# A two-branch decoder layer on one core: single-transfer attention operands, outputs split where they are made, a state update that adds in PSUM

## The chip, the cores and the metric

One core of a Trainium2 chip runs one program. The metric is device time in microseconds, the median of three runs, lower is better. The engines are TensorE (PE: matmuls, with PEld for its weight loads), VectorE (DVE), ScalarE (ACT), GpSimd (POOL), and SyncE (SP), which here only issues DMAs.

## What is computed

One layer on 2048 tokens of width 1024, in float32. A normalised and modulated input goes through one projection (4232 columns). Half of its heads are a recurrence (RWKV-7), half a causal attention with a forget-gate bias. Both are gated and go through one output projection and a second normalisation.

```python
proj = h @ w_in
rw = rw + (rw_prev - rw) * rwkv_mix            # token mix: with the token before
# recurrence, 8 heads of 64, per token t (S is 64x64 per head)
sa = einsum('bhvk,bhk->bhv', S, kk_t)
S = S * w_t - sa * b_t + v_t * k_t             # outer products
y = einsum('bhvk,bhk->bhv', S, r_t)
# attention, 8 heads of 64
s = einsum('bhqd,bhkd->bhqk', qb, kh) * scale + cb[..., None] - cum[:, :, None, :]
p = softmax(where(causal, s, -inf))
# both, then
y = concatenate([y_a, y_b]) * silu(gate)
out = y @ w_out
return layer_norm(alpha * x + (1 + gate_c) * out, ln_g, ln_b)
```

## The kernel before

**Precision.** The large products are taken on operands split in two parts, a rounded high part and the rest (low), with three matmuls (high x high, high x low, low x high) per product; those operands have the type fp32r. The recurrence runs in full float32, where one matmul in the program is two records in the trace.

**Stages.** The sequence is cut into two halves of 1024 tokens, and these into blocks of 512 (`NB`). `proj_stream` runs the projection for a half, tile by tile of 128 output columns (weights arrive by DMA in `wst`, `weights` splits them into `wsp` with one ACT and one POOL instruction). `proc_stream` runs the recurrence and then the attention of each half, while projection matmuls (`ps<-ht,wsp` in the trace) fill PE beside them. At the end the output projection runs over 16 tiles of 128 tokens (`final_tile`, `final_x`, `final_evac`), with its weights' place, `wsp`, now holding the transposed layer output, read back from DRAM (`yscr`).

**Recurrence.** `rwkv_stream` takes 8 units per half (4 pairs of heads by 2 blocks). A unit's 8 chunks of 64 tokens first need a triangular solve (`rwkv_solve`, small matmuls of 32 rows and columns), then `rwkv_batch` (line 1407) runs for two chunks at a time: four matmuls of 128 rows and 128 columns combine the solved factors (`X`) with the right sides (`Z`); ACT and DVE take the result out of PSUM into `Fh` (one half of it through DVE with an addition, the rest copied by ACT). Then, in strict order, each chunk: `mm` for the next state and `mm` for the output, two of each, one per head, and two DVE instructions that scale the new state by `dl`, the chunk's decay, into the other state buffer. A chunk can begin only when the one before has written its state. In `state` each head's 64 rows lie beside a 64x64 identity in the other 64 rows, so that one matmul over 128 rows adds what the chunk itself brings:

```python
for h in range(2):
    i = 2 * h + ci
    mm(b.ap[hs(h), 0:64], Fh[:, i, 64:128], cur[:, h, :])
```

**Attention.** `ev_fox` splits q and k of a block into high and low parts and stores them in DRAM (`qscr`, `kscr`), `ev_f` stores the cumulative forget gates in three parts (`cscr`). `fox_ops` (line 1640) loads the operands of each head and block back with `conv`: each operand (`q1`, `k1`: 64 rows and 3 rows for the bias; `q2`, `k2`: two times 64 rows) is two DMAs into one tile of `fx_s`. `fox_values` loads and transposes the value blocks (`arena<-vscr`). `fox_s` computes scores, `fox_exp` the exponentials, `fox_pv` the products with the values, `fox_out` (line 1853) normalises, gates, and stores an output block in `yscr`; `rwkv_post` (line 1465) does so for the recurrence.

**What sets the order.** The program is written by concurrent generators, and a model of the chip (class `Driver`: `cost`, `on_pe`, `time`) decides which generator issues next, so the modelled durations set the order of all instructions on each engine. The order is fixed when the program is built. All instructions pass through one helper, so all have line 134 in the trace; they are told apart by tile names.

Of the kernel before, what the change touches and what calls it, by code (L numbers as in the profile page):

```python
# [9 lines left out]
F32 = mybir.dt.float32  # L10
# [3 lines left out]
OP = mybir.AluOpType  # L14
# [3 lines left out]
D = 1024  # L18
# [119 lines left out]
class Driver:  # L138
# [31 lines left out]
    def cost(self, e, op, ops, kw):  # L170
# [3 lines left out]
        if "dma_start" in op:  # L174
            return 450.0 if e.name == "sp" else 1000.0
# [35 lines left out]
    def on_pe(self, t, op, ops):  # L211
# [6 lines left out]
        if nr == nc == 4:  # L218
            d = max(stream + (14 if n >= 256 else 3), load + 2)
        else:  # L220
            d = max(stream + (load if nc < 4 else 6), 25.0)
# [113 lines left out]
def hymba_kernel(ctx: ExitStack, tc, x, c, emb_ln_g, emb_ln_b, w_ada, b_ada, w_in, rwkv_mix, w0,  # L335
# [10 lines left out]
    def dap(t, offset, ap):  # L346
# [36 lines left out]
    yscr = [dram.tile([D, TB], F32, name=f"yscr{i}") for i in range(2)]  # L383
    cscr = [dram.tile([3, 8, TB], F32, name=f"cscr{i}") for i in range(2)]
    fscr = [{k: [dram.tile([2, 128, TB] if k in "qk" else [128, TB], F32, name=f"{k}scr{h}{i}") for i in range(4)]
             for k in "qkvg"} for h in range(2)]
    qscr1 = dram.tile([3, 512], F32, name="qscr1")
# [31 lines left out]
    state = const.tile([128, 2, 4, 2, 64], F32, name="state")  # L419
# [156 lines left out]
    def start_consts():  # L576
# [57 lines left out]
        qr = yield from slots.get()  # L634
# [24 lines left out]
        for b in range(2):  # L659
            for p in range(4):  # L660
                dve.tensor_copy(state[64:128, b, p, 0, :], i64[64:128, :])
                dve.tensor_copy(state[0:64, b, p, 1, :], i64[0:64, :])
            yield
# [200 lines left out]
    def weights():  # L864
# [4 lines left out]
        while True:  # L869
# [7 lines left out]
            if k == "out":  # L877
                hf, t0 = divmod(p * 128, TB)
                sp.dma_start(wst[:, 0], dap(yscr[hf], t0, [[TB, 128], [128 * TB, KT], [1, 128]]))
                drv.spawn(final_x(p), 0)  # L880
            else:
                sp.dma_start(wst[:, 0], dap(w_in, c0, [[4232, 128], [128 * 4232, KT], [1, 128]]))
# [64 lines left out]
    def shift_mix(b, g, o):  # L947
# [5 lines left out]
        dve.scalar_tensor_tensor(o[:, 0:1], car[:, g:g + 1], par("mix", g), o[:, 0:1],  # L953
                                 op0=OP.mult, op1=OP.add)
# [11 lines left out]
    def ev_f(b, half, blk):  # L966
# [47 lines left out]
        for t in (z, e, u):  # L1014
            t.free()

# [20 lines left out]
    def ev_fox(k):  # L1037
        def ev(b, half, p, blk):
# [9 lines left out]
            else:  # L1048
# [5 lines left out]
                i = int(k == "q")  # L1054
                sp.dma_start(to[i, :, cols], s.ap)
                yield
                sp.dma_start(to[1 - i, :, cols], l.ap)
                l.free()
            if k in "vg":
                sp.dma_start(to[:, cols], s.ap)  # L1060
# [346 lines left out]
    def rwkv_batch(p, n, c0, bufs, u, qt, yb, dl, st):  # L1407
# [6 lines left out]
        Xh = xs.ap.rearrange("p (i c) -> p i c", c=128)  # L1414
# [13 lines left out]
        for i in range(4):  # L1428
            o = 2 * (i % 2) + i // 2
            mm(b.ap[:, o * 128:(o + 1) * 128], Xh[:, i, :], Z[:, i, :])  # L1430
        yield
        bf = b.ap.rearrange("p (i c) -> p i c", c=128)
        for h in range(2):
            i = slice(2 * h, 2 * h + 2)
            tt(Fh[hs(h), i, 0:64], bf[hs(h), i, 0:64], kr[hs(h), g, 1], OP.add)
            tt(Fh[hs(h), i, 64:128], bf[hs(h), i, 64:128], i64[hs(h), None, :].to_broadcast([64, 2, 64]), OP.add)
        for h in range(2):
            o = hs(1 - h)
            i = slice(2 * h, 2 * h + 2)
            act.activation(Fh[o, i, :], bf[o, i, :], AF.Copy)  # L1440
# [4 lines left out]
        for ci in range(2):  # L1445
# [4 lines left out]
            for h in range(2):  # L1450
                i = 2 * h + ci
                mm(b.ap[hs(h), 0:64], Fh[:, i, 64:128], cur[:, h, :])
            with drv.side():
                for h in range(2):
                    i = 2 * h + ci
                    mm(yb.ap[hs(h), cc * 64:(cc + 1) * 64], cur[:, h, :], Fh[:, i, 0:64])
            yield
            ts(nxt[0:64, 0, :], b.ap[0:64, 0:64], dl[0:64, cc:cc + 1], None, OP.mult)
            ts(nxt[64:128, 1, :], b.ap[64:128, 0:64], dl[64:128, cc:cc + 1], None, OP.mult)
# [3 lines left out]
        st["next"] = (n, c0 + 2) if c0 + 2 < 8 else (n + 1, 0)  # L1463

    def rwkv_post(half, p, blk, yb, bonus):
# [29 lines left out]
        g.free()  # L1495
        yield
        sp.dma_start(yscr[half][p * 128:(p + 1) * 128, blk * NB:(blk + 1) * NB], Y.ap)
        Y.free()
        yield
# [35 lines left out]
    def rwkv_stream(half):  # L1535
# [20 lines left out]
        def elems():  # L1556
            for n in range(8):
# [8 lines left out]
                u.amuse = 2  # L1566
                u.done = done
# [72 lines left out]
    def fox_ops(half, st):  # L1640


        def conv(key, o, H, name, b4):
            while (b4 // 2, H // 2, name[0] + "f", b4 % 2) not in res:
                yield 0
            src = fscr[b4 // 2][name[0]][H // 2]
            c = (b4 % 2) * NB
            if name[1] == "2":
                for i in range(2):
                    sp.dma_start(o.f[hs(i)], src[i, hs(H % 2), c:c + NB])  # L1650
            else:
                sp.dma_start(o.f[0:64], src[int(name == "q1"), hs(H % 2), c:c + NB])
                sp.dma_start(o.f[64:67], cscr[b4 // 2][:, H, c:c + NB] if name == "k1" else qscr1)
# [12 lines left out]
    def fox_guard(half, st):  # L1666
# [15 lines left out]
        def finish(H, qg, mx, left):  # L1682
# [20 lines left out]
            sp.dma_start(ops[H, "q1", qg].f[64:65].rearrange("o (j x) -> o j x", j=4), mrow[0:4, r].bitcast(F32))  # L1703
# [149 lines left out]
    def fox_out(half, p, h, qi, nk, pv, o, sums):  # L1853
# [43 lines left out]
        g.free()  # L1897
        yield
        sp.dma_start(yscr[half][512 + p * 128:640 + p * 128, qi * NB:(qi + 1) * NB], o.ap)
        o.free()  # L1900
        normed[0] += 1
        yield
# [71 lines left out]
    def final_x(i):  # L1974
# [10 lines left out]
        ts(xt.ap, xt.ap, stats[:, i, 0:1], stats[:, i, 1:2], OP.subtract, OP.mult)  # L1985
        yield
        pool.tensor_tensor(xt.ap, xt.ap, fin["eg"].ap, op=OP.mult)
        yield
        tt(xt.ap, xt.ap, fin["eb"].ap, OP.add)
# [115 lines left out]
```

## Time and profile before

| | |
|---|---|
| median of 3 runs | 1868.69 us (1868.56 to 1870.11) |
| profiled execution | 1866.47 us |
| its span | 1864.7 us |
| PE busy | 1784.5 us (96%), 13609 matmul records |
| DVE busy | 1287.4 us (69%) |
| ACT busy | 804.4 us (43%) |
| POOL busy | 779.3 us (42%) |
| DMA | 181.60 MB, mean 97 GB/s |

The span is the time from the first to the last instruction of one profiled execution. Matmuls on PE overlap, so its busy time counts stretches in which at least one is under way, and from start to start of groups is the safer reading of what a group costs. The granted clock is the share of full speed that TensorE was given in a stretch.

### The profile page before, as it was taken

Reading aid. Unit: us, or ns where it says so; the run is one execution under the profiler, and the core shown is the slowest. Engines: PE = TensorE matmul, PEld = TensorE weight load, DVE = VectorE, ACT = ScalarE, POOL = GpSimd, SP = SyncE. Lnnn points to the kernel's source line nnn. Section 1 sums busy time; section 2 is a strip of 40 time slices with the busy share of each in tenths; the row PEclk is TensorE's granted clock in tenths of the full one; section 3 lists DMA queues with packets and bytes.
Section 4 is the critical chain, followed back from the end, with each engine's and each line's share of the span. In section 5 each row is a group of like instructions: output and inputs, shape, how many; then the busy total and the mean of one; then the engine's idle time right before and its main releaser. Section 6 shows DMA issues by size and latency. Waiting matters only on the chain.

```text
span 1864.7 us, 35565 instructions
## 1 busy us (share of the span) xinstructions
PE 1784.5 (96%) x13609; PEld 1288.3 (69%) x13609; DVE 1287.4 (69%) x3049; ACT 804.4 (43%) x1571; POOL 779.3 (42%) x773
## 2 busy tenths in 40 slices
PE   8999999999999899999999999989899899999995
PEld 6777777767777656677777777767555356666884
DVE  4987685665773768667657675762677584876998
ACT  2454555354444245554554554443244344432000
POOL 1333242422423357743143442424256364566652
PEclk8999999998999999999999999999899899999998
DMA  8252020210122755132021120213422732512433
GB/s 263 72 163 81 30 69 23 80 51 26 53 87 86 226 172 178 58 115 84 19 78 36 41 79 30 75 39 114 131 92 84 244 111 77 191 57 90 153 115 122
DMA packets 172129, 181.60 MB, mean 97 GB/s; under 512 B 12180, under 2 KB 116197, under 8 KB 171960
## 3 DMA queue, kind: packets, MB, share of 16 engines
q1 hardware_dynamic: 171960, 179.33, 30.6%
q8 instruction: 108, 1.77, 0.4%
q14 instruction: 61, 0.50, 0.1%
HBM read 132.10 MB, written 47.13 MB: 96 GB/s over the span
## 4 chain that ended last, share of the span: by engine, by line
PE 55%; DVE 5%; ACT 3%; SPq 3%; DMA 2%; issue 2%; POOL 1%; DVEq 0%; ACTq 0%; POOLq 0%
PE ps L134 55%; SPq L134 3%; ACT rw_s L134 2%; DVE rw_s L134 2%; DMA arena<-vscr 1%; DVE end_s L134 1%; DVE small L134 1%; DVE arena L134 1%; POOL rw_s L134 0%; POOL wsp L134 0%; DMA arena<-in_b_ada_dram 0%; ACT arena L134 0%; DMA yscr<-rw_s 0%; DVE fx_p L134 0%; DMA fx_s<-qscr 0%
## 5 line engine op out<-in xcount | busy, mean ns | idle before, releaser
L134 PE MATMUL ps<-ht,wsp 128*128 128x512 f32 x3840 | 976.4, 400 | 3.4 <-POOL wsp L134 1.3
L134 PEld LDWEIGHTS ps<-ht,wsp 128*128 128x128 f32 x3840 | 701.1, 189 | 163.3 <-issue 15.0
L134 POOL TENSOR_TENSOR wsp<-wst,wsp 128x1024 fp32r<-128x1024 f32 x79 | 192.8, 2440 | 320.2 <-ACT wsp L134 256.2
L134 ACT ACTIVATE rw_s<-ps 64x256 f32<-64x256 f32 (+3 forms) x544 | 215.9, 409 | 200.7 <-PE ps L134 101.0
L134 PE MATMUL ps<-fx_s 67*128 67x512 f32 (+6 forms) x960 | 261.1, 390 | 12.3 <-DMA fx_s<-kscr 4.0
L134 ACT ACTIVATE fx_p<-ps 128x512 f32<-128x512 f32 (+3 forms) x336 | 162.8, 521 | 196.2 <-PE ps L134 175.6
L134 PEld LDWEIGHTS ps<-fx_s 67*128 67x128 f32 (+1 forms) x960 | 165.4, 193 | 118.3 <-issue 47.7
L134 POOL TENSOR_TENSOR fx_p<-fx_p 128x512 f32<-128x512 f32 (+2 forms) x160 | 185.7, 1167 | 140.7 <-PE ps L134 138.3
L134 PE MATMUL ps<-rw_s 32*32 32x32 f32 (+4 forms) x5376 | 227.7, 217 | 17.0 <-DVE rw_s L134 8.0
L134 PEld LDWEIGHTS ps<-rw_s 32*32 32x32 f32 (+3 forms) x5376 | 195.7, 130 | 66.1 <-issue 26.6
L134 DVE TENSOR_TENSOR rw_s<-rw_s 128x24 f32<-128x24 f32 (+11 forms) x544 | 179.8, 336 | 26.0 <-ACT rw_s L134 12.6
L134 DVE TENSOR_REDUCE small<-ps 128x1 f32<-128x512 f32 (+1 forms) x208 | 134.5, 683 | 44.4 <-PE ps L134 43.6
L134 ACT ACTIVATE arena<-ps 128x512 f32<-128x512 f32 (+3 forms) x128 | 74.1, 581 | 191.6 <-PE ps L134 161.7
L134 POOL TENSOR_TENSOR small<-small,nhalf 128x8 f32<-128x8 f32 (+1 forms) x48 | 68.3, 1425 | 211.6 <-DVE small L134 211.5
L134 PE MATMUL ps<-fx_p,fx_v 128*64 128x512 f32 (+3 forms) x640 | 155.9, 556 | 0.0
L134 DVE TENSOR_TENSOR fx_p<-fx_p 128x512 f32<-128x512 f32 (+1 forms) x128 | 111.9, 874 | 51.6 <-POOL fx_p L134 48.9
L134 ACT ACTIVATE wsp<-wst 128x1024 fp32r<-128x1024 f32 x80 | 84.3, 1054 | 134.2 <-PE ps L134 110.1
L134 DVE TENSOR_SCALAR state<-ps,dl 64x64 f32<-64x64 f32 x256 | 72.4, 283 | 64.2 <-PE ps L134 57.2
L134 POOL TENSOR_TENSOR rw_s<-rw_s,arena 128x512 f32<-128x512 f32 x64 | 84.9, 1328 | 69.4 <-ACT arena L134 39.2
L134 DVE TENSOR_TENSOR arena<-ps,arena 128x512 fp32r<-128x512 f32 (+4 forms) x108 | 72.5, 677 | 54.0 <-ACT arena L134 50.3
L134 POOL TENSOR_SCALAR rw_s<-rw_s 64x128 f32<-64x128 f32 x128 | 38.0, 297 | 120.0 <-PE ps L134 109.4
L134 ACT ACTIVATE rw_s<-rw_s 32x256 f32<-32x256 f32 (+2 forms) x112 | 70.0, 653 | 39.4 <-DVE rw_s L134 38.7
(152 smaller groups left out, 1864.9 us busy)
## 6 DMA issues: line engine op xcount, KB each, us to landing
wst<-in_w_in_dram SPq DMA_DIRECT2D x66, 512.0 KB
fx_s<-kscr SPq DMA_DIRECT2D x144, 128.0 KB
fx_s<-qscr SPq DMA_DIRECT2D x96, 128.0 KB
ada_t<-in_w_ada_dram SPq DMA_DIRECT2D x16, 512.0 KB
rw_l<-lowscr SPq DMA_DIRECT2D x32, 256.0 KB
kscr<-arena SPq DMA_DIRECT2D x32, 256.0 KB
qscr<-arena SPq DMA_DIRECT2D x32, 256.0 KB
arena<-in_x_dram SPq DMA_DIRECT2D x16, 512.0 KB
```

Source lines behind the costliest of these rows:

```text
L134: return fn(*args, **kw)
```

## The change

It has six parts.

1. *Recurrence.* The identity rows of `state` go; the tile holds both heads in its 128 rows. What a chunk itself brings to the next state is added in PSUM by two matmuls over 128 rows ahead of the two state matmuls, which now read 64 rows each; the new state is scaled by one DVE instruction for both heads. What the batch's tokens bring to the output is put into the output bank by four matmuls of the batch, to which the chunk's output matmuls add. The batch's four matmuls now make 64 output rows each instead of 128, and two DVE instructions take out what four and two of ACT did.
2. *Attention operands.* The DRAM tiles of q and k hold the bias rows and the parts in the order in which an operand needs them, so that each operand is one DMA (160 in place of 320). For that the high part of q is written twice and the cumulative rows are copied from DRAM to DRAM, and operands wait until that is issued (`res[half, "cum", blk]`).
3. *Outputs.* `store_y` splits each finished output block (32 of them) into high and low, one ACT and one DVE instruction, and stores both; the output weights are then loaded by two DMAs straight into `wsp`, once that buffer is free, with no split by ACT and POOL. `final_x` becomes two DVE instructions in place of two on DVE and one on POOL.
4. *Token mix.* The first column of a block goes from DVE to ACT.
5. *State set-up.* 16 DVE copies into `state` at the start go.
6. *Order model.* SP's modelled cost of a DMA is 600 ns for more than 8 partitions (450 before), and a matmul on a part of the array has another modelled duration. These numbers only move the order.

```diff
-            return 450.0 if e.name == "sp" else 1000.0
+            return (450.0 if list(out.ap)[0][1] <= 8 else 600.0) if e.name == "sp" else 1000.0
...
-            d = max(stream + (load if nc < 4 else 6), 25.0)
+            d = max(stream + 6, load + 5, 52.0)
...
-    yscr = [dram.tile([D, TB], F32, name=f"yscr{i}") for i in range(2)]
+    yscr = [dram.tile([2, D, TB], F32, name=f"yscr{i}") for i in range(2)]
...
-    fscr = [{k: [dram.tile([2, 128, TB] if k in "qk" else [128, TB], F32, name=f"{k}scr{h}{i}") for i in range(4)]
-             for k in "qkvg"} for h in range(2)]
-    qscr1 = dram.tile([3, 512], F32, name="qscr1")
+    rowsof = dict(q=[2, 195, TB], k=[2, 131, TB], v=[128, TB], g=[128, TB])
+    fscr = [{k: [dram.tile(rowsof[k], F32, name=f"{k}scr{h}{i}") for i in range(4)] for k in "qkvg"} for h in range(2)]
+    qscr1 = dram.tile([3, TB], F32, name="qscr1")
...
-    state = const.tile([128, 2, 4, 2, 64], F32, name="state")
+    state = const.tile([128, 2, 4, 64], F32, name="state")
...
-        for b in range(2):
-            for p in range(4):
-                dve.tensor_copy(state[64:128, b, p, 0, :], i64[64:128, :])
-                dve.tensor_copy(state[0:64, b, p, 1, :], i64[0:64, :])
-            yield
...
             if k == "out":
                 hf, t0 = divmod(p * 128, TB)
-                sp.dma_start(wst[:, 0], dap(yscr[hf], t0, [[TB, 128], [128 * TB, KT], [1, 128]]))
+                w = yield from wb.get()
+                for i in range(2):
+                    sp.dma_start(w.ap.bitcast(F32)[:, i], dap(yscr[hf], i * D * TB + t0, [[TB, 128], [128 * TB, KT], [1, 128]]))
                 drv.spawn(final_x(p), 0)
+                yield
+                wready.append((it, w))
+                continue
...
-        dve.scalar_tensor_tensor(o[:, 0:1], car[:, g:g + 1], par("mix", g), o[:, 0:1],
-                                 op0=OP.mult, op1=OP.add)
+        act.activation(o[:, 0:1], car[:, g:g + 1], AF.Identity, scale=par("mix", g), bias=o[:, 0:1])
...
+        for p in range(4):
+            sp.dma_start(dap(fscr[half]["k"][p], blk * NB, [[131 * TB, 2], [TB, 3], [1, NB]]),
+                         dap(cscr[half], 2 * p * TB + blk * NB, [[TB, 2], [8 * TB, 3], [1, NB]]))
+            if blk == 0:
+                sp.dma_start(dap(fscr[half]["q"][p], 0, [[195 * TB, 2], [TB, 3], [1, TB]]),
+                             dap(qscr1, 0, [[0, 2], [TB, 3], [1, TB]]))
+            yield
+        res[half, "cum", blk] = True
...
-                i = int(k == "q")
-                sp.dma_start(to[i, :, cols], s.ap)
+                part = lambda r: dap(to, r * TB + blk * NB, [[rowsof[k][1] * TB, 2], [TB, 64], [1, NB]])
+                sp.dma_start(part(3), s.ap)
                 yield
-                sp.dma_start(to[1 - i, :, cols], l.ap)
+                sp.dma_start(part(67), l.ap)
                 l.free()
+                if k == "q":
+                    sp.dma_start(part(131), s.ap)
...
-        for i in range(4):
-            o = 2 * (i % 2) + i // 2
-            mm(b.ap[:, o * 128:(o + 1) * 128], Xh[:, i, :], Z[:, i, :])
-        yield
-        bf = b.ap.rearrange("p (i c) -> p i c", c=128)
-        for h in range(2):
-            i = slice(2 * h, 2 * h + 2)
-            tt(Fh[hs(h), i, 0:64], bf[hs(h), i, 0:64], kr[hs(h), g, 1], OP.add)
-            tt(Fh[hs(h), i, 64:128], bf[hs(h), i, 64:128], i64[hs(h), None, :].to_broadcast([64, 2, 64]), OP.add)
-        for h in range(2):
-            o = hs(1 - h)
-            i = slice(2 * h, 2 * h + 2)
-            act.activation(Fh[o, i, :], bf[o, i, :], AF.Copy)
+        for ci in range(2):
+            for h in range(2):
+                mm(b.ap[hs(h), ci * 128:ci * 128 + 128], X4[:, ci, 192 * h:192 * h + 64], Z[:, 2 * ci + h, :], start=not ci)
+        for ci in range(2):
+            for h in range(2):
+                xv = X4[:, ci, 64 + 64 * h:128 + 64 * h]
+                mm(yb.ap[hs(h), (c0 + ci) * 64:(c0 + ci + 1) * 64], xv, Z[:, 2 * ci + h, 0:64], start=not u.begun[h],
+                   stop=False)
+                u.begun[h] = True
+        yield
+        bf = b.ap[:, 0:256].rearrange("p (i c) -> p i c", c=128)
+        tt(Fh[:, 0:2, 64:128], bf[:, :, 64:128], i64[:, None, :].to_broadcast([128, 2, 64]), OP.add)
+        tt(Fh[:, 0:2, 0:64], bf[:, :, 0:64], kr[:, g, 1], OP.add)
...
             for h in range(2):
-                i = 2 * h + ci
-                mm(b.ap[hs(h), 0:64], Fh[:, i, 64:128], cur[:, h, :])
+                mm(b.ap[hs(h), 0:64], Z[:, 2 * ci + h, 64:128], X4[:, ci, 64 + 64 * h:128 + 64 * h], stop=False)
+            for h in range(2):
+                mm(b.ap[hs(h), 0:64], Fh[hs(h), ci, 64:128], cur[hs(h)], start=False)
             with drv.side():
                 for h in range(2):
-                    i = 2 * h + ci
-                    mm(yb.ap[hs(h), cc * 64:(cc + 1) * 64], cur[:, h, :], Fh[:, i, 0:64])
+                    mm(yb.ap[hs(h), cc * 64:(cc + 1) * 64], cur[hs(h)], Fh[hs(h), ci, 0:64], start=False)
             yield
-            ts(nxt[0:64, 0, :], b.ap[0:64, 0:64], dl[0:64, cc:cc + 1], None, OP.mult)
-            ts(nxt[64:128, 1, :], b.ap[64:128, 0:64], dl[64:128, cc:cc + 1], None, OP.mult)
+            ts(nxt, b.ap[:, 0:64], dl[:, cc:cc + 1], None, OP.mult)
...
+    def store_y(half, c0, blk, y, g):
+
+        act.activation(g.r, y.ap, AF.Copy)
+        yield
+        tt(y.r, y.ap, g.ap, OP.subtract)
+        to = yscr[half]
+        cols = slice(blk * NB, (blk + 1) * NB)
+        sp.dma_start(to[0, c0:c0 + 128, cols], g.ap)
+        g.free()
+        yield
+        sp.dma_start(to[1, c0:c0 + 128, cols], y.ap)
...
         tt(Y.ap, Y.ap, g.ap, OP.mult, pool)
-        g.free()
-        yield
-        sp.dma_start(yscr[half][p * 128:(p + 1) * 128, blk * NB:(blk + 1) * NB], Y.ap)
-        Y.free()
-        yield
+        yield
+        yield from store_y(half, p * 128, blk, Y, g)
...
+            while (b4 // 2, "cum", b4 % 2) not in res:
+                yield 0
             src = fscr[b4 // 2][name[0]][H // 2]
-            c = (b4 % 2) * NB
-            if name[1] == "2":
-                for i in range(2):
-                    sp.dma_start(o.f[hs(i)], src[i, hs(H % 2), c:c + NB])
-            else:
-                sp.dma_start(o.f[0:64], src[int(name == "q1"), hs(H % 2), c:c + NB])
-                sp.dma_start(o.f[64:67], cscr[b4 // 2][:, H, c:c + NB] if name == "k1" else qscr1)
+            r0, n = dict(k1=(0, 67), k2=(3, 128), q1=(0, 67), q2=(67, 128))[name]
+            sp.dma_start(o.f[0:n], src[H % 2, r0:r0 + n, (b4 % 2) * NB:(b4 % 2 + 1) * NB])
...
-            sp.dma_start(ops[H, "q1", qg].f[64:65].rearrange("o (j x) -> o j x", j=4), mrow[0:4, r].bitcast(F32))
+            sp.dma_start(ops[H, "q1", qg].f[0:1].rearrange("o (j x) -> o j x", j=4), mrow[0:4, r].bitcast(F32))
...
-        ts(xt.ap, xt.ap, stats[:, i, 0:1], stats[:, i, 1:2], OP.subtract, OP.mult)
-        yield
-        pool.tensor_tensor(xt.ap, xt.ap, fin["eg"].ap, op=OP.mult)
-        yield
-        tt(xt.ap, xt.ap, fin["eb"].ap, OP.add)
+        dve.scalar_tensor_tensor(xt.ap, xt.ap, stats[:, i, 0:1], fin["eg"].ap, op0=OP.subtract, op1=OP.mult)
+        yield
+        dve.scalar_tensor_tensor(xt.ap, xt.ap, stats[:, i, 1:2], fin["eb"].ap, op0=OP.mult, op1=OP.add)
```

The order of PE shows the recurrence. A row names the PSUM bank and the operands, the output's partitions and columns, and how many follow one another; `32x32`, `64x64` and `64x128` outputs use a part of the array. In the first half's recurrent stage, two chunks before:

```order
L134 MATMUL ps<-rw_s 128x128 x8
L134 MATMUL ps<-ht,wsp 128x512 x12
L134 MATMUL ps<-state,rw_s 64x64 x2
L134 MATMUL ps<-rw_s,state 64x64 x2
L134 MATMUL ps<-ht,wsp 128x512 x6
L134 MATMUL ps<-state,rw_s 64x64 x2
L134 MATMUL ps<-rw_s,state 64x64 x2
L134 MATMUL ps<-ht,wsp 128x512 x3
L134 MATMUL ps<-ident,rw_s 128x128 x4
```

And the same place now:

```order
L134 MATMUL ps<-rw_s 64x128 x4
L134 MATMUL ps<-rw_s 64x64 x4
L134 MATMUL ps<-rw_s 64x128 x4
L134 MATMUL ps<-rw_s 64x64 x6
L134 MATMUL ps<-state,rw_s 64x64 x2
L134 MATMUL ps<-rw_s,state 64x64 x2
L134 MATMUL ps<-ht,wsp 128x512 x3
L134 MATMUL ps<-rw_s 64x64 x2
L134 MATMUL ps<-state,rw_s 64x64 x2
L134 MATMUL ps<-rw_s,state 64x64 x2
L134 MATMUL ps<-ht,wsp 128x512 x3
L134 MATMUL ps<-ident,rw_s 128x128 x4
```

The eight 128x128 matmuls of two batches have become four of 64x128 and four of 64x64 for each batch (the last row of these, x6, holds the first chunk's two as well), and ahead of each chunk's two state matmuls stand two `ps<-rw_s 64x64` that read all 128 rows.

The order of SP at the start of the second half's attention shows the operands. The tiles of `fx_s` are the operands; `qscr`, `kscr` and `cscr` are the parts stored in DRAM; `arena<-vscr` is the value block that PE transposes. Before, the first of its rows:

```order
L134 DMA fx_v<-vscr_109 128x512
L134 DMA arena<-vscr_96 128x512
L134 DMA fx_s<-qscr_88 64x512
L134 DMA fx_s<-qscr_104 3x512
L134 DMA fx_s<-qscr_88 64x512
L134 DMA fx_s<-qscr_104 3x512
L134 DMA fx_s<-kscr_76 64x512
L134 DMA fx_s<-cscr_70 3x512
L134 DMA fx_s<-kscr_76 64x512
L134 DMA fx_s<-cscr_70 3x512
```

Now, from the same place:

```order
L134 DMA fx_v<-vscr_109 128x512
L134 DMA arena<-vscr_96 128x512
L134 DMA fx_s<-qscr_88 67x512 x2
L134 DMA fx_s<-kscr_76 67x512 x2
L134 DMA fx_s<-kscr_92 67x512 x2
L134 DMA fx_s<-qscr_88 128x512 x2
L134 DMA fx_s<-kscr_76 128x512 x2
L134 DMA fx_s<-kscr_92 128x512 x2
```

and further on to the second value block:

```order
L134 DMA fx_s<-qscr_88 128x512 x2
L134 DMA fx_s<-kscr_76 128x512
L134 DMA gscr_102<-arena 128x512
L134 DMA wst<-in_w_in_dram 128x8x128
L134 DMA arena<-vscr_96 128x512
```

Each operand's two rows have become one of 67 or 128 partitions; the second value block follows after 21 operand DMAs where before it followed after 42.

The order of DVE at the end of the program shows the last tiles. `small` are a tile's statistics, `end_s` its values, and `ps` the output bank of the last matmuls. Before:

```order
L134 SCALAR_TENSOR_TENSOR end_s<-end_s,small,arena 128x512 x2
L134 TENSOR_TENSOR small<-small 128x1 x2
L134 SCALAR_TENSOR_TENSOR end_s<-end_s,small,arena 128x512 x3
L134 TENSOR_SCALAR small<-small 128x1
L134 SCALAR_TENSOR_TENSOR end_s<-end_s,small,arena 128x512
L134 TENSOR_TENSOR small<-small 128x1
L134 SCALAR_TENSOR_TENSOR end_s<-end_s,small,arena 128x512 x7
```

Now:

```order
L134 TENSOR_TENSOR end_s<-ps,end_s 128x512
L134 BN_STATS small<-end_s 128x6
L134 SCALAR_TENSOR_TENSOR end_s<-end_s,small,arena 128x512
L134 TENSOR_TENSOR end_s<-ps,end_s 128x512
L134 BN_STATS small<-end_s 128x6
L134 BN_AGGR small<-small 128x2
L134 TENSOR_SCALAR small<-small 128x1
L134 TENSOR_TENSOR small<-small 128x1 x2
L134 TENSOR_SCALAR small<-small 128x1
L134 TENSOR_TENSOR small<-small 128x1
L134 SCALAR_TENSOR_TENSOR end_s<-end_s,small,arena 128x512 x4
```

Before, the last output bank has long been taken out where these rows begin; now the last bank's addition is followed by its own statistics and four multiply-adds, which end the order.

## Rows read from the trace of the kernel before

**Rows 1.** The page: busy time, share of the span and instructions of each engine.

```profile
PE 1784.5 (96%) x13609; PEld 1288.3 (69%) x13609; DVE 1287.4 (69%) x3049; ACT 804.4 (43%) x1571; POOL 779.3 (42%) x773
```

**Rows 2.** Waits of PE over the span: us in total, times, longest us.

```profile
PE ps L134 <- ACT rw_s L134: 10.8, 23, 1.3
PE ps L134 <- DMA arena<-vscr: 10.2, 6, 6.1
```

**Rows 3.** Timeline in the recurrent stage: start us, us, engine, operation, idle before.

```profile
302.33 0.60 DVE L134 TENSOR_SCALAR state<-ps,dl 64x64 f32<-64x64 f32 x2
...
304.30 0.56 PE L134 MATMUL ps<-state,rw_s 128*64 128x64 f32 x3
...
304.97 0.71 PE L134 MATMUL ps<-rw_s 128*128 128x128 f32 x4
305.61 0.34 PE L134 MATMUL ps<-state,rw_s 128*64 128x64 f32 x4
305.77 0.29 PE L134 MATMUL ps<-rw_s,state 128*64 128x64 f32 x4
305.99 0.97 PE L134 MATMUL ps<-ht,wsp 128*128 128x512 f32 x3
```

**Rows 4.** Windows: us, busy of PE, PEld, DVE, ACT, POOL; granted clock, DMA share, GB/s.

```profile
432.00:446.00 14.00, 14.00 (x207) 10.42 (x207) 3.33 (x12) 6.79 (x17) 2.85 (x5) 0.51 0.13 37
1325.30:1331.70 6.40, 0.34 (x3) 0.05 (x1) 0.00 (x0) 0.77 (x1) 0.00 (x0) 0.87 0.85 246
1330.00:1340.00 10.00, 8.32 (x22) 5.12 (x23) 4.27 (x10) 4.26 (x8) 3.22 (x2) 0.50 0.45 139
1844.00:1864.70 20.70, 0.00 (x0) 0.00 (x0) 17.70 (x43) 0.00 (x0) 1.55 (x2) 0.62 0.36 139
```

**Rows 5.** Timeline of PE: runs of full-width matmuls in the recurrent stage.

```profile
215.31 1.95 PE L134 MATMUL ps<-rw_s 128*128 128x128 f32 x16
217.01 3.00 PE L134 MATMUL ps<-ht,wsp 128*128 128x512 f32 x12
...
226.54 1.50 PE L134 MATMUL ps<-rw_s 128*128 128x128 f32 x12
227.79 0.94 PE L134 MATMUL ps<-ht,wsp 128*128 128x512 f32 x3
```

**Rows 6.** Timeline of PE: a run of half-height matmuls of 128 columns.

```profile
143.68 1.16 PE L134 MATMUL ps<-rw_s 64*128 64x128 f32 x16
144.77 1.42 PE L134 MATMUL ps<-ht,wsp 128*128 128x512 f32 x5
```

**Rows 7.** The tile state: its engines idle before its instructions, us and times.

```profile
  ACT rw_s L134: 21.5, 47
  DVE state L134: 9.1, 25
```

**Rows 8.** Timeline of SP, PE and ACT in the second attention stage.

```profile
1300.50 2.02 SPq L134 DMA_DIRECT2D fx_s<-qscr  x4
...
1325.26 0.69 SPq L134 DMA_DIRECT2D arena<-vscr  x1
...
1331.68 1.09 PE L134 MATMUL ps<-ident,arena 128*128 128x128 f32 x4 [6.06 <-DMA arena<-vscr]
...
1458.79 1.06 ACT L134 ACTIVATE arena<-arena 128x1024 f32<-128x1024 f32 x1 [11.95 <-DMA arena<-in_b_ada_dram]
```

**Rows 9.** Timeline of ACT and DVE beside the output tiles.

```profile
1767.65 1.06 ACT L134 ACTIVATE wsp<-wst 128x1024 fp32r<-128x1024 f32 x1 [9.81 <-PE ps L134]
1778.53 1.06 ACT L134 ACTIVATE wsp<-wst 128x1024 fp32r<-128x1024 f32 x1 [9.82 <-PE ps L134]
...
1758.68 2.88 DVE L134 TENSOR_SCALAR end_s<-end_s,stats 128x1024 f32<-128x1024 f32 x1
...
1775.06 0.80 DVE L134 TENSOR_SCALAR end_s<-end_s,stats 128x1024 f32<-128x1024 f32 x1
```

**Rows 10.** The tile end_s from 1846 on: duration ns min/median/max, first and last start.

```profile
L134 DVE SCALAR_TENSOR_TENSOR end_s<-end_s,small,arena x21: 699/744/752, 1846.7 to 1861.0; 128x512 f32<-128x512 f32 x21
```

More of the change, by code (lines that the diff above doesn't have):

```diff
@@ L633, in start_consts @@
             yield
-        qr = yield from slots.get()
+        qr = yield from slots.get(2)
         pool.memset(qr.ap[0:3], 1.0)
@@ L1413, in rwkv_batch @@
         X4 = xs.ap.rearrange("p (c i) -> p c i", i=256)
-        Xh = xs.ap.rearrange("p (i c) -> p i c", c=128)
         Fh = q.ap.rearrange("p (i c) -> p i c", c=128)
@@ L1463, in rwkv_batch @@
         st["next"] = (n, c0 + 2) if c0 + 2 < 8 else (n + 1, 0)
+    def store_y(half, c0, blk, y, g):
[8 more added lines that the diff above has]
+        sp.dma_start(to[1, c0:c0 + 128, cols], y.ap)
+        y.free()
+        yield
     def rwkv_post(half, p, blk, yb, bonus):
@@ L1566, in elems @@
                 u.amuse = 2
+                u.begun = [False, False]
                 u.done = done
@@ L1896, in fox_out @@
         tt(o.ap, o.ap, g.ap, OP.mult, pool)
-        g.free()
         yield
-        sp.dma_start(yscr[half][512 + p * 128:640 + p * 128, qi * NB:(qi + 1) * NB], o.ap)
-        o.free()
+        yield from store_y(half, 512 + p * 128, qi, o, g)
         normed[0] += 1
-        yield
         ystored[half] += 1
```

## The prediction

> **What bounds the kernel now.** The page's engine table comes first: TensorE (PE) is busy 96% of the span, every other engine at most 69% [rows 1]. Such a kernel can gain from two things only: less time that PE needs for its own instructions, or less time in which it stands still. So everything below is asked of PE. What the change takes off VectorE (DVE), ScalarE (ACT) and GpSimd (POOL) counts only where PE, or the end of the span, waits for it.
>
> The waits of PE come second. The two longest sums of the span are 10.8 us for ACT in the recurrent stage and 10.2 us, in only six waits, for the load of the value block in attention [rows 2]. These are idle times of an engine whose matmuls overlap; a matmul that waits while the one before it still counts as busy does not show there. The timeline of PE shows it: a chunk's eight records (state update and output, two passes for each fp32 matmul) take 0.38 us from their start to the next start when nothing is late (305.61 to 305.99), and 0.67 us (304.30 to 304.97) when the state is [rows 3].
>
> The windows come third, for the clock: PE ran at a granted 0.51 for 14 us from 432 on and at 0.50 for 10 us from 1330 on, the lower of its two levels (1.2 GHz), the second time behind a stop [rows 4].
>
> The end comes last. From 1844.0 to the span's end at 1864.7 PE runs nothing; DVE is busy 17.7 of these 20.7 us, and the last store follows [rows 4].
>
> **Part 1, the recurrent chunks: more PE work.** Per chunk (128 of them) two matmuls are added ahead of the state update; they are four records. Four such records take 0.16 us (305.61 to 305.77 [rows 3]), so 128 x 0.16 = **+20.5 us**. The second four take 0.22 with a change of tiling behind them; half of that and all of it are my bounds, 14 and 28.
>
> Per batch (64) four full-width matmuls of 128 columns become four of half the array's width and the same columns, and four output matmuls of 64 columns are new. Runs of 16 and of 12 full-width records take 1.70 and 1.25 us to the next start [rows 5], a difference of 0.112 for each, so 8 records are 0.90 us. Sixteen half-height records of 128 columns take 1.09 us with one change of tiling [rows 6]; without it, 0.06 each, so 8 are 0.50. Eight of 64 columns are a chunk's 0.38 less one change, 0.28. So 0.78 against 0.90: 64 x -0.12 = **-7.4 us**; bounds -12 and 0, since half-width records of 128 columns don't occur before.
>
> The two orders differ in one more thing: the array's tiling (128x128, 128x64, 64x64 and so on) changes 1035 times before and 1201 times after, counted in the two orders, +166. 128 of these lie inside a chunk, where the added matmuls use all 128 rows and the state matmuls now 64. Price: the four full-width records at 304.97 stand between two groups of another tiling and take 0.64 us to the next start, against 4 x 0.112 = 0.45 [rows 3], so two changes cost 0.19. I take 0.10 for one: **+16.6 us**; bounds 0.06 (the 0.22 against the 0.16 above, 10 us) and 0.19 (were all of it the price of one, 31 us). Against the usual advice to split small matmuls over the array stands a rule of the Trainium skill, "TensorEngine Tiling (Array Packing)", section Key Properties: changing the mode drains the engine, using another tile of the same mode does not. The trace agrees, with the 0.10 us just read. By the isolated-matmul constant of the Trainium skill's "TensorE: Matmul & The Clock Gate", section Single matmul latency (166 ns warm), an estimate for the 166 changes would be 27.6 us, and the whole sum would come out 4 us above no change.
>
> **Part 2, the recurrent chain: shorter.** The state is now one DVE instruction for both heads instead of two; the two took 0.60 us together [rows 3], so the second head's matmul is released about 0.3 us sooner. Of the batch's evacuation two ACT copies go and four DVE additions become two. Before the state's instructions their engine sat idle 21.5 us for ACT and 9.1 us for DVE [rows 7], part of it under a running matmul. I take about a third, **-11 us**; bounds 0 (other work is late in its place) and -16. The other waits of that stage (most of the 10.8 for ACT [rows 2]) and the 7 us that the lower clock from 432 on cost [rows 4] are due to the triangular solve, which the change does not touch; its engines are less loaded, so **-5 us**, bounds 0 and -15.
>
> **Part 3, attention operands.** Each operand is one DMA instead of two. At the start of the second attention stage SP issues 42 DMAs into operands, one behind the other, from 1300.50 on, and only at 1325.26 the load of the second value block; PE stands 6.06 us for it [rows 8]. That load now comes behind 21 such issues. The bytes are the same, and DMA already moved 246 GB/s while PE stood [rows 4], so issue time halves but transfer time doesn't. PE's waits for such loads sum to 10.2 us [rows 2], and the lower clock behind the stop cost 5 (10 us at 0.50 [rows 4]). I take two thirds of the 15, **-10 us**; bounds 0 and -15. New behind this: operands wait for the cumulative rows, copied DRAM to DRAM. These are written long before the stage starts, so nothing; SP waits some us for them four times, under weights that are loaded ahead.
>
> **Part 4, the output split.** ACT and DVE now split each output block where it is made (32 more instructions for each), and ACT and POOL no longer split the 16 output weights. Those splits lay beside a PE that paced the tail at 10.88 us a tile (1767.65 to 1778.53 [rows 9]). Each tile's weights now go as 1 MB straight into their buffer once it is free; at the 246 GB/s above that is 4.3 us, inside those 10.88. So no PE time. But POOL leaves the tail, and DVE with it catches up: the same instruction of DVE took 0.80 us and, with POOL at work, 2.88 [rows 9], which is how DVE fell behind. After the last matmul it still ran 21 multiply-adds from 1846.7 on, 0.7 us each [rows 10]; four belong to the last tile. In the new order only these four follow. 17 x 0.7 = 12 less, about 1 for the inverse root on POOL, which was covered by them: **-11 us**; bounds -6 and -12.
>
> **Edits at nothing.** The token-mix column (52 instructions) goes from DVE to ACT; 16 DVE copies into the state at the start go; DVE and ACT there are not waited for.
>
> **Sum.** +20.5 - 7.4 + 16.6 - 11 - 5 - 10 - 11 = -7.3 us. From the profiled execution's 1866.5 us that gives 1859.2. The median of the runs is 2.2 us above that execution, so the prediction is 1868.7 - 7.3 = **1861.4 us**.
>
> **Rivals.**
> *Tiling changes cost more.* If entering the smaller tiling costs the whole 0.19, 166 of them are 31.5 us, 15 more than I take: **1876 us, slower**. The sign turns at 0.10 + 7.3 / 166 = 0.14. For it: the first records of a new tiling cannot have their weights loaded under the old one. Against: a chunk's 0.38 us already hold one change. Chance 0.18.
> *The stall of the attention start moves.* The load of the gate's bias now stands at the second start; before, ACT waited 11.95 us for it, up to 1458.79, and held up the exponentials behind it [rows 8]. If PE stops there for as long as before, the 10 us are gone: **1871 us, no change**. Chance 0.14.
> *The stalls go wholly.* At the far bounds of the chain, the solve and the starts (-16, -15, -15), 20 less: **1841 us**. Against: PE has few filler matmuls in the second attention stage. Chance 0.18.
>
> **Numbers.** My forecast has 0.50 (1850 to 1871). What a measurement of this kernel can tell from no change is about 0.2%, 3.7 us, so faster is below 1865.0 and slower above 1872.4. Faster: 0.42 of the forecast's 0.50 and the third rival, 0.60. Same: the rest of the forecast and most of the second rival, 0.20. Slower: the first rival and the second's edge, 0.20. The range from 1838 to 1878 takes in all four; what it leaves out are sums with two terms at their far bounds.
>
> **What would show it.** Right: PE ends some 10 us before the span; the 6.06 us wait is gone; the chunk takes about 0.65 us with 12 records. Wrong: a chunk above 0.8 us (tiling), a stop of PE near the second attention start for the bias, or PE idle between output tiles.

## The result, and the profile after

The changed kernel takes **2309.28 us** (median of 4 runs, 2308.76 to 2320.0) against 1868.62 in the same comparison: a ratio of 1.237, 95% interval 1.2333 to 1.2406. It is 441 us slower, where the forecast was 7 us faster.

The page's engine table of the changed kernel, to be read beside [rows 1]:

```profile
PE 1898.8 (82%) x14633; PEld 1346.2 (58%) x14633; DVE 1194.2 (52%) x2757; ACT 776.5 (34%) x1511; POOL 686.0 (30%) x741
```

PE no longer paces the kernel: it is busy 82% of the span, not 96%, and stands idle 409 us (2307.4 - 1898.8) where it stood 80. The waits of PE over the span (us in total, times, longest) say for what, beside [rows 2]:

```profile
PE ps L134 <- DMA fx_s<-kscr: 172.3, 16, 18.5
PE ps L134 <- DMA arena<-vscr: 74.6, 7, 34.1
PE ps L134 <- DVE rw_s L134: 25.4, 5, 7.7
PE ps L134 <- ACT rw_s L134: 17.7, 13, 6.8
...
PE ps L134 <- DMA fx_s<-qscr: 14.2, 1, 14.2
```

172.3 + 74.6 + 14.2 = 261 us are waits for the operands that the change made single transfers, and for the value block queued behind such transfers on SP; the rest of the idle time that came new are other waits that grew. A second part goes with the clock, behind the stops: PE's busy time rose by 114 us, though as many matmuls with mended transfers (below) take only 8 us more than before; the mean granted clock is 0.888 here and 0.988 there, 0.980 before.

The timelines of SP and PE at the start of the first attention stage (start us, us, engine, operation, idle before):

```profile
659.69 10.69 SPq L134 DMA_DIRECT2D fx_s<-kscr  x2
670.42 5.52 SPq L134 DMA_DIRECT2D fx_s<-qscr  x2
...
662.74 1.12 PE L134 MATMUL ps<-ident,arena 128*128 128x128 f32 x4 [10.21 <-DMA arena<-vscr]
...
679.31 1.09 PE L134 MATMUL ps<-fx_s 67*128 67x128 f32 x3 [14.18 <-DMA fx_s<-qscr]
```

The first row is two loads of 67 rows, the second two of 128. Two issues on SP take 10.69 us where four took 2.02 in [rows 8]. The windows of the same place show what moves meanwhile (us; busy of PE, PEld, DVE, ACT, POOL; granted clock, DMA share, GB/s):

```profile
648.50:653.50 5.00, 4.02 (x18) 3.00 (x16) 0.31 (x1) 0.77 (x2) 2.39 (x1) 1.00 0.13 47
661.00:676.00 15.00, 2.40 (x7) 1.58 (x7) 0.00 (x0) 0.66 (x2) 0.00 (x0) 0.50 0.07 27
```

The DMA share is the mean over 16 engines, so it can be read as a count: 0.07 x 16 is about one engine, at work for 15 us on end while the others stand, and 27 GB/s is what it carries. An operand of 67 rows of 2 KB is 137 KB, 5.1 us at that rate, which is SP's time for one of the two long issues. In the first window, where stores of k are under way (`kscr<-arena`), 0.13 x 16 is two engines. The mean alone can't tell one busy engine from many that are seldom busy; the experiments do. The granted clock of the second window is 0.50, the lower level.

Two signs of the forecast are there all the same. The chunk now, from the timeline of PE, beside [rows 3]:

```profile
224.09 0.34 PE L134 MATMUL ps<-rw_s 128*64 128x64 f32 x4
224.36 0.33 PE L134 MATMUL ps<-state,rw_s 64*64 64x64 f32 x4
224.52 0.28 PE L134 MATMUL ps<-rw_s,state 64*64 64x64 f32 x4
224.74 0.97 PE L134 MATMUL ps<-ht,wsp 128*128 128x512 f32 x3
```

Twelve records take 0.65 us, and the added four with their change of tiling 0.27. And the end, beside the last row of [rows 4]:

```profile
2298.20:2307.40 9.20, 0.00 (x0) 0.00 (x0) 5.21 (x12) 0.00 (x0) 0.55 (x1) 0.69 0.15 57
```

The last matmul is followed by 9.2 us, not 20.7.

### The profile page after: what moved, and what is told of

Its sections match the earlier page's. It is cut to its first block, busy times and chain, and to the rows that moved or that the text cites. A ratio compares the mean times of both kernels' runs of the same rounds, so it can differ in the third digit from the quotient of the medians.

```text
span 2307.4 us, 36957 instructions
## 1 busy us (share of the span) xinstructions
PE 1898.8 (82%) x14633; PEld 1346.2 (58%) x14633; DVE 1194.2 (52%) x2757; ACT 776.5 (34%) x1511; POOL 686.0 (30%) x741
## 4 chain that ended last, share of the span: by engine, by line
PE 60%; DMA 23%; SPq 7%; DVE 4%; ACT 4%; issue 2%; POOL 0%; POOLq 0%; ACTq 0%; DVEq 0%
PE ps L134 60%; DMA fx_s<-kscr 8%; SPq L134 7%; DMA kscr<-arena 3%; DMA fx_s<-mrow 3%; DMA wst<-in_w_in_dram 2%; DMA arena<-vscr 2%; ACT rw_s L134 2%; DMA qscr<-arena 2%; DVE arena L134 2%; ACT arena L134 1%; DMA yscr<-rw_s 1%; DMA yscr<-arena 1%; DVE small L134 1%; DVE rw_s L134 0%
## 5 line engine op out<-in xcount | busy, mean ns | idle before, releaser
L134 PE MATMUL ps<-ht,wsp 128*128 128x512 f32 x3840 | 1001.7, 408 | 2.8 <-POOL wsp L134 1.4
L134 PE MATMUL ps<-fx_s 67*128 67x512 f32 (+6 forms) x960 | 296.1, 430 | 225.2 <-DMA fx_s<-kscr 172.3
L134 PEld LDWEIGHTS ps<-fx_s 67*128 67x128 f32 (+1 forms) x960 | 187.6, 218 | 359.1 <-issue 256.4
L134 PE MATMUL ps<-rw_s 32*32 32x32 f32 (+6 forms) x6400 | 259.7, 223 | 39.0 <-DVE rw_s L134 25.4
L134 PEld LDWEIGHTS ps<-rw_s 32*32 32x32 f32 (+4 forms) x6400 | 208.8, 129 | 127.2 <-issue 66.6
L134 POOL TENSOR_TENSOR wsp<-wst,wsp 128x1024 fp32r<-128x1024 f32 x63 | 151.8, 2409 | 423.6 <-ACT wsp L134 414.8
L134 ACT ACTIVATE rw_s<-ps 32x256 f32<-32x256 f32 (+3 forms) x416 | 169.4, 418 | 175.6 <-PE ps L134 158.3
L134 DVE CUSTOM_DVE_ANT_0 ps<-ps,mneg 128x128 f32<-128x128 f32 (+3 forms) x128 | 62.2, 503 | 175.2 <-PE ps L134 174.8
L134 DVE TENSOR_TENSOR arena<-ps,arena 128x512 f32<-128x512 f32 (+4 forms) x108 | 73.1, 679 | 130.3 <-ACT arena L134 78.0
L134 PE MATMUL ps<-ident,arena 128*128 128x128 f32 (+1 forms) x197 | 37.5, 324 | 84.8 <-DMA arena<-vscr 74.6
```

The source lines that it names most:

```text
L134: return fn(*args, **kw)
```

## Experiments: the transfers

Theory A: a transfer uses only as many of the 16 DMA engines as divide its outermost sizes on both sides. 67 rows are prime, so one engine; the stores of q and k have an outermost 2 (two heads), so two. Theory B: the issue on SP is long by itself. Theory C: the loss is in the recurrence. The runs with 80, 68 and 77 rows, with the stores alone and with the operands alone are one execution each; executions of one kernel differ here by up to 1%, some 20 us.

**80 rows in place of 67.** The operand's tile takes the next 13 rows of the same DRAM tile with it; no matmul reads them.

```diff
+            n = 80 if n == 67 else n
             sp.dma_start(o.f[0:n], src[H % 2, r0:r0 + n, (b4 % 2) * NB:(b4 % 2 + 1) * NB])
```

> The changed kernel, but each operand of 67 rows is loaded as 80 rows (the 13 more are the next rows of the same DRAM tile, not used). Theory A: a transfer is spread over as many of the 16 DMA engines as divide its outermost row counts, so 67 rows run on one engine at the 26 GB/s that the changed kernel's trace shows (5.3 us each, 80 of them) and its stores of q and k with a leading 2 on two engines at some 50 GB/s. Then most of the 441 us goes: 1880 to 2050 us, the stores still slow. Theory B: the issue of these DMAs on SP is itself long, by the rows that it describes: 80 rows cost more than 67, 2309 us or more. Theory C: the loss is in the recurrence (tiling changes): no change, 2300 to 2320.

Measured: 1986.76 us. More bytes, and 323 us less. Theories B and C fall.

**68 rows.** The same line with 68.

> As the run with 80 rows, with 68 rows in its place. Theory A: 68 divides by 4 of up to 16, so a load runs on four engines at about 100 GB/s (1.4 us): most of the loss goes here too, 0 to 80 us above the run with 80 rows. Theory B (SP's issue by rows) and theory C (recurrence): 2300 to 2320 us.

Measured: 2043.42 us, 57 above the 80 rows. A window of such loads (a load of 128 rows is issued behind them at 655.03):

```profile
653.00:656.00 3.00, 0.00 (x0) 0.00 (x0) 0.00 (x0) 0.00 (x0) 0.00 (x0) 0.50 0.26 90
```

0.26 x 16 is four engines, at 90 GB/s. One row more than the changed kernel, and three times the rate.

**Stores of 64 rows.** Loads as changed, each of the 80 stores of a part of q or k as two.

```diff
-                part = lambda r: dap(to, r * TB + blk * NB, [[rowsof[k][1] * TB, 2], [TB, 64], [1, NB]])
-                sp.dma_start(part(3), s.ap)
+                for h in range(2):
+                    sp.dma_start(to[h, 3:67, cols], s.ap[hs(h)])
```

(and so for the rows from 67 and from 131.)

> The changed kernel, but each store of a part of q or k (two heads of 64 rows, 80 such DMAs, with a leading dimension of 2) is two DMAs of 64 rows. Theory A: a store goes from two engines to all 16, from some 5.2 us to 0.7 of transfer time; the loads of 67 rows stay on one: 2150 to 2300 us. Theory B: 80 more issues on SP, so 2309 to 2350. Theory C: no change.

Measured: 2168.18 us, 141 less, with twice the issues. The stores are a second part of the loss, as theory A has it.

**Both.** 80 rows and stores of 64.

> Loads of 80 rows and stores of 64 rows together, all else as in the changed kernel. Theory A: the whole loss lay in these two, and what is left is the sum forecast for the rest of the change: 1861 us, 1840 to 1880. Theory B: above 2300. Theory C: about 2309, as the recurrence is as changed.

Measured: **1834.51 us**, ratio 0.982 (0.979 to 0.9849). The loss is gone and the kernel is faster than before, by more than was forecast and outside what was expected here. Its engine table, its waits of PE, and the window of its operand loads:

```profile
PE 1792.4 (98%) x14633; PEld 1287.0 (70%) x14633; DVE 1202.3 (66%) x2757; ACT 775.7 (42%) x1511; POOL 698.9 (38%) x741
```

```profile
PE ps L134 <- ACT rw_s L134: 5.4, 11, 0.7
PE ps L134 <- DMA ada_t<-in_w_ada_dram: 4.7, 2, 3.9
PE ps L134 <- DVE rw_s L134: 3.3, 3, 1.5
PE ps L134 <- DMA fx_s<-kscr: 3.2, 2, 2.5
...
PE ps L134 <- DMA arena<-vscr: 1.1, 2, 0.9
```

```profile
600.00:606.00 6.00, 5.19 (x26) 3.86 (x25) 2.36 (x8) 1.25 (x3) 0.00 (x0) 1.00 0.92 273
```

The wait for kscr went from 172.3 to 3.2 us, that for the value block from 74.6 to 1.1 (10.2 before the change), and the loads run on nearly all engines (those of 128 rows are in this window too).

**77 rows.** Does the rule count divisors, or powers of two?

> The 1834.5 us kernel with loads of 77 rows in place of 80. 77 is odd, but divides by 11. Theory A (the largest number up to 16 that divides the rows): eleven engines, some 285 GB/s in the loads, and no loss: 1828 to 1845 us. Rival A2, that only powers of two count (67 and 77 odd: one engine; 68: four; 80: sixteen): as with 67 rows and stores of 64, 2150 to 2190 us.

Measured: 1834.62 us, as with 80. A window in a run of such loads, in the second attention stage:

```profile
1314.00:1316.00 2.00, 2.00 (x12) 1.69 (x11) 1.57 (x6) 0.00 (x0) 0.00 (x0) 1.00 0.73 187
```

The share is near 11/16 = 0.69, and far from one engine's 0.06. The neighbouring windows of 2 us, with loads of 128 rows among them, have 0.77 to 1.03, so that it is exactly eleven is not shown; that 77 rows don't run on one engine is. An odd count did no harm here, where it has a large divisor up to 16.

**The operands' part alone on the kernel before.** All hunks of operands (layout, cumulative rows, stores, loads), nothing else.

> The kernel before with the operands' part of the change alone: 67 rows in one DMA, stores with a leading 2. Theory A, that this part alone holds the loss: +400 to +480 us on 1866, so 2270 to 2350. If the loss needs the rest of the change too (a recurrence that leaves less cover): below 2200.

Measured: 2357.28 us, 488 above before, a little over what was expected. The waits of PE:

```profile
PE ps L134 <- DMA fx_s<-kscr: 191.6, 17, 25.5
PE ps L134 <- DMA arena<-vscr: 75.3, 7, 35.5
```

This part alone makes the loss, and undoing it alone in the mended kernel (below) gives no loss either.

## Experiments: the rest of the change

With the transfers mended the change gives -33 us, the forecast was -7. So each part but the token mix was undone in the 1834.5 us kernel.

**Recurrence undone** (state of two heads beside an identity, two scalings).

> The kernel with loads of 80 rows and stores of 64 rows (1834.5 us), its recurrence as before: two heads beside an identity, two DVE scalings, no adding in PSUM. By the forecast's terms the recurrent part cost +13.7 us (+20.5 - 7.4 + 16.6 of PE work, -11 and -5 of waits), so without it some 1821. Theory D, that the waits it removes were undersized (the state's instructions idled 30.6 us behind ACT and DVE before, under 2 after): the part is a gain, and without it 1845 to 1865.

Measured: 1837.14 us, ratio 0.984 (0.9805 to 0.9876), not to be told from 0.982. Neither expectation. The waits of the tile `state` (its engines idle before its instructions; us, times) are there again, without a loss in the total:

```profile
  ACT rw_s L134: 14.1, 42
...
  DVE state L134: 9.2, 21
```

**Outputs undone** (stored whole; weights split at the end; `final_x` with POOL).

> The 1834.5 us kernel with the outputs as before: stored whole, output weights split by ACT and POOL at the end, three instructions with one on POOL in the last stage. By the forecast's term (-11, all at the end of the span): 1845. Theory D does not touch it. Rival: the DVE and POOL time that it frees in the attention stages matters as well: 1850 or more.

Measured: 1858.46 us, ratio 0.9942 (0.9926 to 0.9958), some 23 us. Half of it is the end: 20.8 us follow the last matmul, as before the change, where the 1834.5 us kernel has 9.2.

**Order model undone.**

```diff
-            return (450.0 if list(out.ap)[0][1] <= 8 else 600.0) if e.name == "sp" else 1000.0
+            return 450.0 if e.name == "sp" else 1000.0
...
-            d = max(stream + 6, load + 5, 52.0)
+            d = max(stream + (load if nc < 4 else 6), 25.0)
```

> The 1834.5 us kernel with the two numbers of the order model as before. The forecast gave them nothing: 1831 to 1838. Rival: the gain over the forecast is one of order, the modelled cost of small matmuls and of SP's DMAs: 1845 to 1862.

Measured: 1853.24 us, ratio 0.9918 (0.9896 to 0.9939). The forecast's nothing was 19 us.

**Operands undone** (two DMAs each, as before).

> The changed kernel with the attention operands stored and loaded as before (two DMAs each), the rest as changed. Theory A, that the operands' layout alone holds the loss: 1834 plus what one transfer for each operand gains. By the forecast that is 10 us, so 1844; rival, the single transfers gain nothing: 1832 to 1837.

Measured: 1841.64 us, ratio 0.9852 (0.9836 to 0.9869). About 7 us for the single transfers, with intervals that touch: between nothing and the forecast's 10.

**The two numbers apart**, the first hunk above alone, then the second alone.

> The 1834.5 us kernel with the modelled cost of a DMA on SP as before (450), the matmul model as changed. With both undone it was 1853.2. If the order is better because the model now knows SP's issues: about 1850. If it is the matmul model: 1831 to 1838.

Measured: 1831.81 us, ratio 0.9826 (0.9804 to 0.9847). SP's number makes no difference that can be told.

> The 1834.5 us kernel with the modelled duration of small matmuls as before, SP's cost as changed. If the matmul model made the 19 us: about 1850, with DVE and ACT waits before the small matmuls of the recurrence. If it is SP's: 1831 to 1838.

Measured: 1845.4 us, ratio 0.99 (0.9878 to 0.9923). The 11 us point to the matmul model, but the small moves below spread by more; what is shown is the wait that was expected. The tile `state` in this kernel:

```profile
  DVE state L134: 16.1, 20
  DVE rw_s L134: 9.7, 10
```

and in the 1834.5 us kernel:

```profile
  ACT arena L134: 0.9, 2
  DVE state L134: 0.7, 4
```

**Small moves of the numbers**, which say nothing new of the chip (52 is the least modelled duration of a small matmul, 600 the modelled issue of a DMA on SP, both in ns): 52 to 56 and 600 to 580; 52 to 48; 52 to 60 and 600 to 620.

> The 1834.5 us kernel with both model numbers moved a little, 52 to 56 and 600 to 580, which tells what a change of order is worth that says nothing new of the chip. If the order's gain is that of a better model: 1831 to 1838. If orders differ by chance: up to 20 us away.

> The 1834.5 us kernel with 52 moved to 48 in the matmul model, 600 kept. If orders differ by chance by some 10 to 20 us whenever a number moves: anywhere from 1815 to 1850. If the numbers as changed are near an optimum that the first small move (1821) only followed further up: 1835 to 1850.

> The 1834.5 us kernel with 52 moved to 60 and 600 to 620. By chance: 1815 to 1850. If a larger number in the matmul model is better by itself, as 56 was: 1821 or less.

Measured: **1821.05** (ratio 0.9766, 0.9746 to 0.9785), 1833.64 (0.982) and 1846.93 (0.9883, 0.9847 to 0.9919). Each of these moves writes another order, and these orders differ by 26 us from best to worst. The first is the fastest kernel of this study, 45 us ahead of the kernel before (1866.45 in that comparison). All three are faster than the kernel before; but the 7, 11 and 19 us of the operands, the matmul model and both numbers, and the 11 us of the outputs that are not the end, lie inside this spread, so the times alone don't credit them to those parts.

**The parts alone on the kernel before.**

> The kernel before with the recurrence's part alone. The forecast's terms for it sum to +13.7 us: 1880. Theory D (its waits were worth more than I took): 1855 to 1866, and the idle time ahead of the state's instructions that was behind ACT and DVE gone. With another order by chance, 12 us either way.

> The kernel before with the outputs' part alone. The forecast: -11, 1855, with 9 us after the last matmul in place of 20.8 and the matmuls ending where they did (1844). If it frees something ahead of the end too, as its undoing suggested (-23): 1843 to 1848 with the last matmul some 10 us sooner.

> The kernel before with the two model numbers alone. The forecast: 0, 1863 to 1870. If the matmul model is better by itself, as its undoing suggested (-11 to -19): 1847 to 1856. If it is right only for the changed recurrence, or its gain was chance: 1860 to 1880.

Measured: recurrence 1889.26 us, ratio 1.0103 (1.0069 to 1.0137); outputs 1878.99, 1.0057 (1.0036 to 1.0078); order model 1884.64, 1.0088 (1.0058 to 1.0119). All slower, by 20, 10 and 15 us. With the outputs' part the end is 9.2 us as forecast, but the last matmul ends at 1868.1 where it was 1844.0. With the recurrence's part alone, the tile `state` waits for:

```profile
  DVE state L134: 23.1, 16
  ACT rw_s L134: 1.8, 2
```

The 21.5 us behind ACT of [rows 7] are gone, as forecast; those behind DVE rose from 9.1 to 23.1. That this comes from the order that the old matmul model writes is shown by the pair above, where that model alone was put back: 16.1 and 0.7. With the changed recurrence they are at most 5.5 under the new model, in every order tried. The new model alone, on the old recurrence, leaves the ACT waits as they were:

```profile
  ACT rw_s L134: 21.5, 44
...
  DVE state L134: 6.2, 17
```

So for these waits the two parts belong together: the recurrence takes the ACT waits away, the model the DVE waits. For the time of the kernel this isn't shown: with the recurrence undone, and 23 us of these waits back, it was 1837.14.

## Why the prediction was wrong

**The step that failed** is part 3: "The bytes are the same, and DMA already moved 246 GB/s while PE stood [rows 4], so issue time halves but transfer time doesn't." It took the rate of a window of transfers of 64 and 128 rows for transfers of 67, and set the bounds of the term at 0 and -15. (The bytes are the same for the loads only; q's high part is stored twice.) No row of the trace before showed a transfer of 67 rows or one with an outermost 2, so nothing there excluded a loss, and the bound above zero that such a price needs was left out. The stores' new layout got no price at all, and none of the rivals was of this kind: the one on the slower side was the tiling's. Measured, for the 80 loads: one engine at 27 GB/s in the window above; for the 80 stores: two; +441 us in the whole and +488 for this part alone. The Trainium skill states the rule, in "DMA: Bandwidth & Descriptors", section Why a DMA increments its semaphore by 16 and not by 1: a transfer uses the largest number of engines up to 16 that divides the outermost sizes (other than 1) of both sides. The runs agree at four places: a DMA share of 0.07 for 67 rows (one of 16 is 0.06), 0.13 for an outermost 2, 0.26 for 68 rows, 0.73 in a window of 77. Weighed at the forecast, that page would have named this rival.

**The term of part 1** held where it can be read: 0.27 us added for each chunk against 0.26 forecast, so the rival of dearer tiling changes falls for the 128 chunks; the other changes of tiling were not read. It is not one chunk alone: from a chunk's first record to the next group's start the median of all 128 is 0.382 us before and 0.643 in the changed kernel.

**Part 2** named the right waits, and for the chunks its size too: the times of the 128 chunks just named sum to 60.5 us before and 82.4 now, 21.9 more, where 128 x 0.261 alone would be 33.4 more; so 11.5 us of lateness are gone, against the 11 forecast. It did not see that this depends on the order: the old model, with the recurrence's part alone, gives 23.1 us behind DVE in the place of 21.5 behind ACT.

**The stall of the second value block** did go once transfers were mended (10.2 to 1.1 us), and it did not move to the gate's bias: PE's waits in the 1834.5 us kernel name no such load (ACT still waits 8.5 us for it once). In the kernel as changed the waits for value blocks grew to 74.6.

**Part 4's end** came to 11.6 us (20.8 to 9.2) against 11, with the four multiply-adds that were forecast.

**"Edits at nothing"**: the two model numbers were not among them nor anywhere in the sum, and their effect was 19 us one way (undone) and 15 us the other (alone). Three moves that carry no information gave 1821 to 1847.

**The -33 of the mended kernel is no success of the sum either.** PE's idle time fell there by 42 us (80.2 to 37.8), where the four savings sum to -37; its busy time rose by 8 (1784.5 to 1792.4), where the three terms of work sum to +29.7. In the chunks that work did come, as just read, so other busy time shrank. The mean granted clock rose from 0.980 to 0.988, by an estimate 0.8% of 1790 or 14 us. Which edit raised it stays open; two of the small moves run at 0.994 and 0.989, so the order alone moves it too. A sum of terms of 5 to 20 us for a kernel whose order a model writes anew with each edit can't be better than that spread; which single waits made the outputs and the order model slower when alone was not taken apart and stays open.

## What to carry to other kernels

Before two transfers become one, look at the row counts and at the outermost size on both sides: read the DMA share times 16 in a window as the number of engines at work, and pad 67 rows to 80, at 19% more bytes, rather than leave them prime (323 us here). Two halves of 64 rows were faster than one transfer with an outermost 2 (141 us for 80 stores). Where a model of the chip writes the order, try a few neutral moves of its numbers before a difference of 10 to 25 us is credited to an edit.

## What was not expected of the hardware

One transfer too narrow holds up more than itself: SP's issue behind it takes some 5 us instead of 0.5, also where that one is wide (the first of the two loads of 128 rows at 670.42 took 5.04). Behind the stops of PE the granted clock is lower (0.50 in the window above), and PE's busy time is 106 us longer than for as many matmuls in the 1834.5 us kernel (1898.8 against 1792.4).
